# Issuing the split of a feed-forward unit's second weights with priority

## The chip, the cores and the metric

The kernel runs on one core of one Trainium2 chip. The metric is the device time of one launch in microseconds. A core has a matrix engine (PE, which loads weights in a queue of its own, PEld, beside its matmuls), two elementwise engines (DVE, the vector engine, and ACT, the scalar engine), POOL (GpSimd) and SP (which issues DMAs here). Each engine works through its own instructions in order, and semaphores join them.

## The reference, cut to what matters

Two decoder layers over 512 tokens of width 1024. Each layer has a feed-forward unit, a token mixer (differential attention in the first layer, causal pooling in the second), a cross-attention into 256 memory tokens, and a second feed-forward unit; a layer norm follows each. So there are four feed-forward units:

```python
def swiglu_ffn(x, w_in, w_out):
    h = x @ w_in                      # (512, 1024) @ (1024, 5632)
    g, u = jnp.split(h, 2, axis=-1)
    return (jax.nn.silu(g) * u) @ w_out   # (512, 2816) @ (2816, 1024)

x = layer_norm(a * x + 0.5 * swiglu_ffn(x, ffn_w_in[i, 0], ffn_w_out[i, 0]), ...)
```

All is in float32. The change touches the feed-forward units alone.

## The kernel before, in words

**Numbers in two halves.** PE multiplies numbers of a rounded format (fp32r). An operand is split in two: ACT casts it to the high half (`wh` for weights), DVE subtracts that from the operand and writes the low half (`wl`). A product is three matmuls per block (`mm3`): high by high (L230), then the low half of the activations by the high weights or the like (L231), then the low weights (L232). So the third matmul of a product needs DVE's `wl`, while the first two need only ACT's `wh`. The pairs `wh`/`wl` have four buffers, handed out in turn.

**A feed-forward unit** (`ffn`) works through eleven blocks of 256 hidden columns in five turns (`FFN_TURNS`): three blocks in the first turn, two in each of the others. The blocks of a turn are called lanes. Each 2 x 2 block product of a lane (`up`) is computed with seven products in place of eight, in the manner of Strassen. Its results stand in PSUM banks `x`, `y` and `z`. The first product of a lane takes the weights `ra` and goes to `x`; the second takes the weights `rc` and goes to `y`; the third takes `ra` again, which POOL's accumulating DMA has turned into a sum by then, and goes to `z`; and so on. ACT copies `x` to `sp`, and DVE adds `y` to it (`hr`, L819).

Beside the lanes of a turn run the products of the way down (`down`) of two blocks of an earlier turn: `b` weights are split like the others (L142, L143), the activations are `ha` and `hb` (`seven` makes them of `hr`, with the sums `sr` in L883 to L886), the results stand in banks `px` and `py`, and DVE adds them to the tokens (`X<-X,px`, L930), which frees the bank. Each tag of banks has two.

`up`, `down` and the rest are generators. `ffn` advances them in turn, so that the program's text order is lane by lane within a step. The recording layer then places the instructions on each engine in an order that it works out from this text order, the dependencies and its priorities. A block under `tc.high_priority()` ranks ahead of what was recorded earlier and is not placed yet; `issue_after` holds an instruction behind a given one.

In `up`, `operand` makes the split of a raw tile: the cast in L742, the subtraction in L744. The variable `v2` holds the split of the second weights, `rc`. In a unit's first turn, lane 0 makes it early, ahead of its first product (`early > 1`); every other lane makes it at the point where `y` begins. `at_start` is true in the first turn of the kernel's first unit only.

Of the kernel before, what the change touches and what calls it, by code (L numbers as in the profile page):

```python
# [125 lines left out]
class Trunk:  # L126
# [592 lines left out]
    def up(self, w, u, lane, early, between):  # L719
# [11 lines left out]
        def load(tag, *block):  # L731
            t = self.raw_tile((4, H), tag)
            self.last_load = nc.sync.dma_start(t, source(*block))
            return t
# [4 lines left out]
        def operand(raw, *behind):  # L739
            v = self.hl([P, 4, H])  # L740
            with self.after([act for act, _ in behind]):
                hi = nc.scalar.copy(v[0], raw)  # L742
            with self.after([dve for _, dve in behind]):
                lo = nc.vector.tensor_sub(v[1], raw, v[0].bitcast(F32))  # L744
            splits.append((hi, lo))
            return v
# [30 lines left out]
        third = lane == 2  # L777
        at_start = early > 0 and self.begins is None
# [5 lines left out]
        rc = load("rc", 2, 1)  # L784
# [11 lines left out]
        v2 = early > 1 and operand(rc, *((self.turned,) if at_start else ()))  # L796
# [8 lines left out]
        nc.scalar.copy(p1, x)  # L805
        yield
        y = bank(self.aux("y", yz))
        v2 = v2 or operand(rc, *((self.made_parts,) if third and at_start else ()))
        with self.behind() if at_start else nullcontext():
            if early > 1 and not at_start:  # L810
                wide = v2[0][:, :2].rearrange("p k n -> p (k n)")
# [988 lines left out]
```

## Time and profile before

| | |
|---|---|
| median of 3 runs | 1905.58 us (1904.58 to 1907.38) |
| the profiled execution | 1907.98 us, its span 1906.2 us |
| PE busy | 1892.1 us (99%), 13136 matmuls |
| weight loads busy | 1733.3 us (91%) |
| DVE busy | 1549.4 us (81%) |
| ACT busy | 1004.8 us (53%) |
| granted clock of PE | 0.999 of full speed |

The times of rows count from the span's start. A matmul's shown duration is longer than its share of PE, since matmuls overlap: how fast PE goes is read from the distance of starts. The four feed-forward units lie in about the first 305 us, from 737 to 1062 us, from 1062 to 1388 us, and from 1574 us to the end.

### The profile page before, as it was taken

What the parts mean: (1) busy time and instruction counts of PE and PEld (TensorE: products, weight loads), DVE (VectorE), ACT (ScalarE), POOL (GpSimd) and SP (SyncE); (2) the same over time, 40 slices, a digit from 0 to 9 for tenths busy, and PEclk for the clock granted to TensorE, in tenths of its full rate; (3) what the DMA queues carried; (4) which work ended last, traced back from release to release, by engine and by line L of the source; (5) the groups of instructions that cost most, each with busy time, mean ns of one, the idle gap of its engine ahead of it and who ended that gap; (6) DMA issues with size and microseconds to landing.
All of it is one profiled execution on the core that took longest, in us unless ns stands there. A gap on an engine that the chain in (4) does not pass through costs nothing.

```text
span 1906.2 us, 32584 instructions
## 1 busy us (share of the span) xinstructions
PE 1892.1 (99%) x13136; PEld 1733.3 (91%) x13136; DVE 1549.4 (81%) x2250; ACT 1004.8 (53%) x1546; POOL 318.0 (17%) x274
## 2 busy tenths in 40 slices
PE   9999999999999999999999999999999999999998
PEld 8999998888889988999998999999899889999996
DVE  7888989888876558889887988898797568998886
ACT  6555553566654436555554655555455436555552
POOL 3112120111210002221220311212130012211210
PEclk9999999999999999999999999999999999999999
DMA  9978772322225327987784687878344438867861
GB/s 250 216 166 185 166 143 89 103 67 70 97 67 177 111 66 185 192 177 166 149 185 165 121 178 166 182 165 184 101 133 136 143 75 178 179 154 169 188 132 54
DMA packets 246871, 277.96 MB, mean 146 GB/s; under 512 B 8384, under 2 KB 212672, under 8 KB 246720
## 3 DMA queue, kind: packets, MB, share of 16 engines
q0 software_dynamic: 92928, 92.29, 31.5%
q1 hardware_dynamic: 153792, 183.59, 29.8%
q8 instruction: 103, 1.69, 0.3%
q14 instruction: 48, 0.39, 0.1%
HBM read 273.75 MB, written 2.10 MB: 145 GB/s over the span
## 4 chain that ended last, share of the span: by engine, by line
PE 88%; DVE 8%; DMA 2%; ACT 1%; issue 1%; POOL 0%; SPq 0%; DVEq 0%; ACTq 0%; POOLq 0%
PE x L230 7%; PE x L231 7%; PE x L232 7%; PE z L230 4%; PE z L231 4%; PE z L232 4%; PE ps L230 4%; PE ps L232 4%; PE ps L231 4%; PE px L230 2%; PE px L232 2%; PE px L231 2%; PE y L232 2%; PE x L769 2%; PE y L230 2%; PE y L231 2%
## 5 line engine op out<-in xcount | busy, mean ns | idle before, releaser
L737 POOL DMA_DIRECT2D ra<-in_ffn_w_in_dram x132 | 170.7, 1314 | 983.1 <-DVE wl L744 824.7
L742 ACT CAST wh<-ra 128x1024 fp32r<-128x1024 f32 x176 | 185.1, 1053 | 209.6 <-PE x L231 68.3
L744 DVE TENSOR_TENSOR wl<-ra,wh 128x1024 fp32r<-128x1024 f32 x176 | 214.0, 1220 | 67.5 <-ACT wh L742 67.1
L230 PE MATMUL x<-xe,wh 128*128 128x256 f32 x704 | 195.1, 277 | 0.0
L231 PE MATMUL x<-xe,wh 128*128 128x256 f32 x704 | 195.0, 277 | 0.0
L232 PE MATMUL x<-xe,wl 128*128 128x256 f32 x704 | 194.9, 277 | 0.0
L742 ACT CAST wh<-rc 128x1024 fp32r<-128x1024 f32 x132 | 139.0, 1053 | 102.6 <-PE x L231 41.6
L142 ACT CAST wh<-b 128x1024 fp32r<-128x1024 f32 x112 | 117.8, 1052 | 132.9 <-PE x L231 68.0
L744 DVE TENSOR_TENSOR wl<-rc,wh 128x1024 fp32r<-128x1024 f32 x132 | 159.9, 1219 | 25.1 <-ACT wh L742 25.1
L143 DVE TENSOR_TENSOR wl<-b,wh 128x1024 fp32r<-128x1024 f32 x112 | 136.7, 1220 | 41.3 <-ACT wh L142 41.3
L230 PE MATMUL x<-xh,wh 128*128 128x256 f32 x536 | 148.8, 278 | 0.0
L231 PE MATMUL x<-xl,wh 128*128 128x256 f32 x536 | 148.4, 277 | 0.0
L232 PE MATMUL x<-xh,wl 128*128 128x256 f32 x536 | 148.4, 277 | 0.0
L231 PEld LDWEIGHTS x<-xe,wh 128*128 128x128 f32 x704 | 132.3, 188 | 1.3
L230 PEld LDWEIGHTS x<-xe,wh 128*128 128x128 f32 x704 | 132.1, 188 | 1.3
L232 PEld LDWEIGHTS x<-xe,wl 128*128 128x128 f32 x704 | 132.6, 188 | 0.0
L143 DVE TENSOR_TENSOR wl<-raw,wh 128x1024 fp32r<-128x1024 f32 x64 | 81.4, 1281 | 42.8 <-ACT wh L142 42.2
L231 PEld LDWEIGHTS x<-xl,wh 128*128 128x128 f32 x536 | 100.8, 188 | 0.7
L230 PEld LDWEIGHTS x<-xh,wh 128*128 128x128 f32 x536 | 100.6, 188 | 0.7
L232 PEld LDWEIGHTS x<-xh,wl 128*128 128x128 f32 x536 | 100.9, 188 | 0.0
L142 ACT CAST wh<-raw 128x1024 fp32r<-128x1024 f32 x64 | 66.6, 1050 | 60.8 <-PE xq L231 16.8
L230 PE MATMUL z<-xe,wh 128*128 128x256 f32 x352 | 97.6, 277 | 0.0
(447 smaller groups left out, 6261.8 us busy)
## 6 DMA issues: line engine op xcount, KB each, us to landing
ra<-in_ffn_w_in_dram POOLq DMA_DIRECT2D x132, 512.0 KB, 6.8
rc<-in_ffn_w_in_dram SPq DMA_DIRECT2D x88, 512.0 KB, 5.7
b<-in_ffn_w_out_dram SPq DMA_DIRECT2D x76, 512.0 KB, 4.8
ra<-in_ffn_w_in_dram SPq DMA_DIRECT2D x44, 512.0 KB, 4.7
rc<-in_ffn_w_in_dram POOLq DMA_DIRECT2D x44, 512.0 KB, 6.8
raw<-in_xa_wkv_dram SPq DMA_DIRECT2D x16, 1024.0 KB, 5.5
raw<-in_da_w_qkv_dram SPq DMA_DIRECT2D x24, 512.0 KB, 3.7
raw<-in_xa_wq_dram SPq DMA_DIRECT2D x8, 1024.0 KB, 5.2
```

The source lines that it names most:

```text
L142: self.nc.scalar.copy(hi, src),
L143: self.nc.vector.tensor_sub(lo, src, hi.bitcast(F32)),
L230: self.first_mm = mm(out, w[0], x[0], start=start, stop=False, skip_group_check=again)
L231: mm(out, w[0], x[1], start=False, stop=False, skip_group_check=again)
L232: self.last_mm = mm(out, w[1], x[0], start=False, stop=stop, skip_group_check=again)
L737: nc.gpsimd.dma_start(t, source(*block), accum_op=ALU.add)
L742: hi = nc.scalar.copy(v[0], raw)
L744: lo = nc.vector.tensor_sub(v[1], raw, v[0].bitcast(F32))
L769: self.last_mm = nc.tensor.matmul(ps[:, j], v[i][:, k, j * P : (j + 1) * P], x[l][:, k], start=n == i == l == 0, stop=n == 7 and i == 1, s ...
```

## The change

The split of `rc` (cast and subtraction) that a lane makes where its `y` begins is recorded under `high_priority()`, except in the first turn of the first unit. Nothing else is touched.

```diff
         y = bank(self.aux("y", yz))
-        v2 = v2 or operand(rc, *((self.made_parts,) if third and at_start else ()))
+        with self.tc.high_priority() if not v2 and not at_start else nullcontext():
+            v2 = v2 or operand(rc, *((self.made_parts,) if third and at_start else ()))
         with self.behind() if at_start else nullcontext():
```

In `up`, `early` is 0 in all turns but the first, where it is 2, 1 and 1 for the three lanes; `at_start` inside `up` is `early > 0 and self.begins is None`, which holds in the first unit's first turn. The added line moves the later lines of the file down by one (L819 becomes L820, L930 becomes L931). SP's and POOL's instructions stand in the same order as before.

The rows below are the order in which the engines' instructions stand in the program; numbers behind names tell buffers apart. The place is the turn that begins near 188 us of the profile, the fourth of the first unit. `rc_1947` and `rc_1951` are the second weights of its two lanes, `wl_2319` and `wl_2351` the low halves of their splits, `y_2317` and `y_2349` their results.

DVE before, from the last `hb` of the turn before to the first `hr` of this one:

```order
L914 TENSOR_TENSOR b1_1953<-b1_1953,b3_1957 128x1024
L143 TENSOR_TENSOR hb_2156<-hr_1724,hb_2155 128x256
L143 TENSOR_TENSOR hb_2156<-sr_2159,hb_2155 128x1024
L744 TENSOR_TENSOR wl_2319<-rc_1947,wh_2318 128x1024
L883 TENSOR_TENSOR sr_2205<-hr_1756 128x256
L886 TENSOR_TENSOR sr_2205<-hr_1756 128x256
L884 SCALAR_TENSOR_TENSOR sr_2205<-sr_2205,hr_1756 128x256
L930 SCALAR_TENSOR_TENSOR X0_74<-X0_74,px_2301 128x512
L885 SCALAR_TENSOR_TENSOR sr_2205<-sr_2205,hr_1756 128x256
L930 SCALAR_TENSOR_TENSOR X1_75<-X1_75,px_2309 128x512
L744 TENSOR_TENSOR wl_2351<-rc_1951,wh_2350 128x1024
L819 TENSOR_TENSOR hr_2346<-y_2317,sp_2262 128x2x256
```

DVE now, at the same place, from eight rows further up:

```order
L931 SCALAR_TENSOR_TENSOR X2_76<-X2_76,px_1679 128x512
L143 TENSOR_TENSOR hb_1580<-sr_1583,hb_1579 128x1024
L744 TENSOR_TENSOR wl_2319<-rc_1947,wh_2318 128x1024
L143 TENSOR_TENSOR hb_1580<-hr_1119,hb_1579 128x256
L744 TENSOR_TENSOR wl_2351<-rc_1951,wh_2350 128x1024
L884 TENSOR_TENSOR sr_2159<-hr_1724 128x256
L887 TENSOR_TENSOR sr_2159<-hr_1724 128x256
L885 SCALAR_TENSOR_TENSOR sr_2159<-sr_2159,hr_1724 128x256
L931 SCALAR_TENSOR_TENSOR X3_77<-X3_77,px_1687 128x512
L886 SCALAR_TENSOR_TENSOR sr_2159<-sr_2159,hr_1724 128x256
L915 TENSOR_TENSOR b1_1953<-b1_1953,b3_1957 128x1024
L143 TENSOR_TENSOR hb_2156<-hr_1724,hb_2155 128x256
```

The two subtractions have moved up, the first by nine rows and the second by fourteen; the rows between them and the common `hr_2346` are the same, one or two 1024-wide rows later.

PE before, at the border of the two lanes' `y`:

```order
L231 MATMUL y_2317<-xl_86,wh_2318 128x256
L232 MATMUL y_2317<-xh_84,wl_2319 128x256
L230 MATMUL y_2349<-xh_84,wh_2350 128x256
L231 MATMUL y_2349<-xl_86,wh_2350 128x256
L230 MATMUL py_2385<-wh_2381,ha_1577 128x512
L232 MATMUL y_2349<-xh_84,wl_2351 128x256
```

PE now, at the end of the second lane's `y`:

```order
L230 MATMUL y_2349<-xh_84,wh_2350 128x256
L231 MATMUL y_2349<-xl_86,wh_2350 128x256
L232 MATMUL y_2349<-xh_84,wl_2351 128x256
L230 MATMUL py_2385<-wh_2381,ha_1577 128x512
L231 MATMUL py_2385<-wl_2382,ha_1577 128x512
```

The one `py` matmul that stood ahead of the second lane's first low product now stands with the other `py` matmuls, behind all of that lane's `y`. PE's order changes in this way at eight places (the third and the fourth turn of each unit) and nowhere else.

ACT before, in the same turn:

```order
L142 CAST hb_1579<-sr_1583 128x1024
L142 CAST hb_1579<-hr_1119 128x256
L742 CAST wh_2318<-rc_1947 128x1024
L142 CAST hb_2155<-hr_1724 128x256
L742 CAST wh_2350<-rc_1951 128x1024
L805 COPY sp_2262<-x_2237 128x512
L142 CAST hb_2155<-sr_2159 128x1024
L142 CAST wh_2381<-b2_1955 128x1024
```

ACT now:

```order
L142 CAST hb_1579<-sr_1583 128x1024
L742 CAST wh_2318<-rc_1947 128x1024
L142 CAST hb_1579<-hr_1119 128x256
L142 CAST hb_2155<-hr_1724 128x256
L742 CAST wh_2350<-rc_1951 128x1024
L805 COPY sp_2262<-x_2237 128x512
L142 CAST wh_2381<-b2_1955 128x1024
L142 CAST hb_2155<-sr_2159 128x1024
```

The first cast of `rc` has passed one small row, and the cast of `hb` that needs DVE's `sr_2159` has gone behind the cast of `b2`.

## The prediction

> **What bounds the kernel now.** I read the page's first and fourth part, then the waits of the weight loads, then the chain of waits, and last the timelines around each place that it names.
>
> ```profile
> span 1906.2 us, 32584 instructions
> ...
> PE 1892.1 (99%) x13136; PEld 1733.3 (91%) x13136; DVE 1549.4 (81%) x2250; ACT 1004.8 (53%) x1546; POOL 318.0 (17%) x274
> ...
> PE 88%; DVE 8%; DMA 2%; ACT 1%; issue 1%; POOL 0%; SPq 0%; DVEq 0%; ACTq 0%; POOLq 0%
> ```
>
> PE is busy for 99% of the span, and 88% of the chain that ended last is PE itself. A change that removes no matmul can win only what PE loses between matmuls. The 8% of DVE in the chain is not such a loss: while the chain runs through DVE, PE goes on with matmuls that it has ready. The loss itself stands in the list of waits, of the weight loads (who waited <- for whom: total us, times, longest), and the chain says where DVE is last (start, us, what; the first and the last of seven such rows, one for each of the seven waits):
>
> ```profile
> PEld y L232 <- DVE wl L744: 3.2, 7, 0.5
> PEld q L230 <- issue: 2.6, 7, 0.4
> ...
> 199.47 1.15 DVE wl L744
> ...
> 1760.30 1.14 DVE wl L744
> ```
>
> The first row is the largest wait of the weight loads, and it is the one that the change is about: the low half `wl` of the second lane's `rc` weights comes too late for its `y`. It bounds what can be won there: 3.2 us, 0.17% of the span. It includes the time in which the previous matmul still runs, so the true loss is read from the starts of PE's matmuls (timeline: start, us, engine, line, operation) at the first and the last place:
>
> ```profile
> 200.01 0.28 PE L231 MATMUL y<-xl,wh 128*128 128x256 f32 x1
> 200.13 0.39 PE L230 MATMUL py<-wh,ha 128*128 128x512 f32 x1
> 200.66 0.19 PEld L232 LDWEIGHTS y<-xh,wl 128*128 128x128 f32 x1 [0.46 <-DVE wl L744]
> 200.66 0.39 PE L232 MATMUL y<-xh,wl 128*128 128x256 f32 x1
> 200.89 0.28 PE L230 MATMUL y<-xh,wh 128*128 128x256 f32 x1
> ...
> 203.36 0.40 PE L231 MATMUL py<-wl,ha 128*128 128x512 f32 x1
> 203.59 0.40 PE L232 MATMUL py<-wh,ha 128*128 128x512 f32 x1
> ...
> 1760.84 0.28 PE L231 MATMUL y<-xl,wh 128*128 128x256 f32 x1
> 1760.96 0.39 PE L230 MATMUL py<-wh,ha 128*128 128x512 f32 x1
> 1761.49 0.38 PE L232 MATMUL y<-xh,wl 128*128 128x256 f32 x1
> 1761.71 0.28 PE L230 MATMUL y<-xh,wh 128*128 128x256 f32 x1
> ```
>
> From start to start, a 256-column matmul takes 0.12 us (200.01 to 200.13; 0.11 at 1760.84) and a 512-column one 0.23 (203.36 to 203.59). So the `y` at 200.66 could have started at 200.13 + 0.23 = 200.36: 0.30 us late. It then takes 0.23 to the next start instead of 0.11 to 0.12, since its weight load starts with it (200.66, released by DVE's `wl`): another 0.11. At the last place it is 1761.49 - 1761.19 = 0.30, and 0.22 - 0.11 = 0.11. The eighth place, the first unit's third turn, just makes it:
>
> ```profile
> 142.52 0.40 PE L230 MATMUL py<-wh,ha 128*128 128x512 f32 x1
> 142.76 0.36 PE L232 MATMUL y<-xh,wl 128*128 128x256 f32 x1
> 142.96 0.28 PE L230 MATMUL y<-xh,wh 128*128 128x256 f32 x1
> ```
>
> There the wait is 0.24 - 0.23 = 0.01, and the slow restart 0.20 - 0.11 = 0.09.
>
> **The change part by part.** It adds and removes no instruction, and SP's and POOL's orders are the same in both programs, so no DMA is issued past another. Under priority now are 38 pairs of a cast (ACT) and a subtraction (DVE): two in each of the sixteen later turns, two in each of the three first turns that are not the first unit's. They make four kinds of place.
>
> *Middle turns (third and fourth of each unit, eight places).* DVE's and ACT's rows of before, and the PE matmul that needs the bank that DVE frees:
>
> ```profile
> 189.48 1.05 ACT L742 CAST wh<-rc 128x1024 fp32r<-128x1024 f32 x1
> 191.02 1.06 ACT L742 CAST wh<-rc 128x1024 fp32r<-128x1024 f32 x1 [0.18 <-ACT hb L142]
> ...
> 189.70 1.22 DVE L143 TENSOR_TENSOR hb<-sr,hb 128x1024 fp32r<-128x1024 f32 x1
> 190.84 0.42 DVE L143 TENSOR_TENSOR hb<-hr,hb 128x256 fp32r<-128x256 f32 x1
> 192.18 0.68 DVE L930 SCALAR_TENSOR_TENSOR X<-X,px 128x512 f32<-128x512 f32 x1
> 195.72 1.22 DVE L744 TENSOR_TENSOR wl<-rc,wh 128x1024 fp32r<-128x1024 f32 x1
> 199.39 1.22 DVE L744 TENSOR_TENSOR wl<-rc,wh 128x1024 fp32r<-128x1024 f32 x1
> 200.53 0.68 DVE L819 TENSOR_TENSOR hr<-y,sp 128x512 f32<-128x512 f32 x1
> 201.13 1.21 DVE L143 TENSOR_TENSOR wl<-b,wh 128x1024 fp32r<-128x1024 f32 x1
> ...
> 195.78 0.39 PE L230 MATMUL px<-wh,ha 128*128 128x512 f32 x1
> ```
>
> Both casts are long done (192.08) when DVE comes to the second subtraction at 199.39: DVE's order, not ACT, makes `y` wait. In the new order the two subtractions stand right behind `hb<-sr` of 189.70 and behind `hb<-hr` of 190.84. A 1024-wide row occupies DVE for 1.14 (189.70 to 190.84), so the first runs 190.84 to 191.98 and ends its write at 192.06; `hb<-hr`, 0.34; the second starts at 192.32 (its cast ends at 192.08, 0.24 earlier) and ends at 193.54. PE reads it at 200.13 at the earliest: 6.6 us of slack in place of a wait of 0.30.
>
> What is paid: everything between is later by 2 x 1.14 = 2.28 at first. The first that PE needs is the `X<-X,px` of 192.18: it starts at 194.46 and ends at 195.14, and the product that reuses its bank starts at 195.78, so 0.64 us are left. The small `sr` and `hb` rows feed products of the next turn. ACT's second `hb<-sr` cast now stands behind a `wh<-b` and needs DVE's later `sr`; its product also belongs to the next turn. At 200.53 both orders have the same rows behind them, and DVE has had no gap, so `hr<-y` and `wl<-b` stay where they are. `wl<-b` ends at 201.13 + 1.21 = 202.34. PE wants it at 203.36, and 0.41 earlier now: 0.61 left. I cost the move at nothing here; the two covers are 0.64 and 0.61 us, and each is the next to be late.
>
> *Second turn of each unit (four places).* Here the splits stood early enough, and PE's order does not change. The first row that both orders have in common again is the `wl<-ra` of 84.27; ahead of it stands now the last `X<-X,px`, at 84.27 - 0.60 (the step from 200.53 to 201.13) = 83.67. Its bank is written next at 111.43. Nothing.
>
> ```profile
> 84.27 1.21 DVE L744 TENSOR_TENSOR wl<-ra,wh 128x1024 fp32r<-128x1024 f32 x1
> ...
> 111.43 0.40 PE L230 MATMUL px<-wh,hb 128*128 128x512 f32 x1
> ```
>
> *Last turn of each unit (four places).* One subtraction moves up by two rows' worth of `sr`, and ACT's `wh<-ra` of 252.58 goes behind a cast of 1.05 and a copy of 0.58:
>
> ```profile
> 251.27 1.05 ACT L142 CAST hb<-sr 128x1024 fp32r<-128x1024 f32 x1 [0.67 <-DVE sr L885]
> 252.58 1.06 ACT L742 CAST wh<-ra 128x1024 fp32r<-128x1024 f32 x1 [0.26 <-PE x L231]
> 256.04 0.68 DVE L819 TENSOR_TENSOR hr<-y,sp 128x512 f32<-128x512 f32 x1
> 257.89 0.28 PE L230 MATMUL z<-xh,wh 128*128 128x256 f32 x1
> ```
>
> The `sr` before the cast waits for the moved 1.14, so the cast starts near 252.4, the copy near 253.4, and `wh<-ra` near 253.9, ending about 255.0. DVE took that operand at 254.90, so `hr<-y` at 256.04 slips by 0.1. `z` at 257.89 needs its end (256.72): 1.0 us left. Nothing.
>
> *First turn of the second to fourth unit.* In the second and third unit the third lane's subtraction (748.04) goes ahead of two rows, which slip by 1.14. `xl<-pt` of 746.31 then ends near 748.1, and the `y` that waits for its bank starts at 751.07. In the fourth unit some five rows change places; I take nothing there and bound it by one wait of the kind above, 0.4 us:
>
> ```profile
> 746.31 0.68 DVE L143 TENSOR_TENSOR xl<-pt,xh 128x512 fp32r<-128x512 f32 x1
> 748.04 1.22 DVE L744 TENSOR_TENSOR wl<-rc,wh 128x1024 fp32r<-128x1024 f32 x1
> 751.07 0.28 PE L230 MATMUL y<-xh,wh 128*128 128x256 f32 x1
> ```
>
> **The sum.** Seven places at 0.30 + 0.11 = 0.41 make 2.9 us, the eighth 0.1: 3.0 us. Bounds of a place: nothing (the wait is replaced by another) and 0.46, the wait of the weight load. The profiled execution took 1907.98 us around its span of 1906.2; it becomes 1905.0. It stands 2.4 above the median of the runs, so against 1905.58 the forecast is 1902.6, 0.16% less.
>
> The restart term is where a rule differs. The Trainium skill, "TensorE: Matmul & The Clock Gate", section "Architectural detail", says that PE's queue can pull weight loads ahead of matmuls in flight; read so, a restart should cost nothing, and the sum would be 7 x 0.30 = 2.1. The trace does not agree at these places: the weight load of 200.66 reads the very `wl` that is awaited, and it starts with its matmul. I keep 0.11.
>
> **The rivals.**
> - *The stall only moves.* DVE is without a gap across the whole stretch, so what is put back may be late in its turn: `X<-X,px` or `wl<-b`. For it: covers of 0.64 and 0.61 us only, and two rows of 1.14 pass. Against it: both covers come out positive by rows. If one is eaten and a wait of about the old size appears, the time is 1905.6.
> - *Slower, by the bank of `px`.* If a further 1024-wide row (1.14) gets ahead of the `X` read, or a cast is that late, PE waits 1.14 - 0.64 = 0.50 and restarts for 0.11, at eight places: 4.9 us lost against 3.0 won, 1907.5. It decides from 0.64 + 0.27 = 0.9 us of lateness (8 x 0.38 = 3.0). The cast that DVE needs at 192.32 has only 0.24 to spare, which speaks for it; against it speaks that the same rows stand ahead of that cast on ACT as before.
> - *The restart is free.* Then only the waits go: 2.1 us, 1903.5. The rows at 200.66 and 1761.49 speak against it.
> - *More is won.* Operands freed earlier could also shorten waits that the change does not aim at, such as the `q` row in the list (2.6 us). To pass 0.2% it must add 0.8 us; no row of a feed-forward unit promises that. 1901.5.
>
> **How the numbers follow.** Forecast 0.55, stall moves 0.17, slower by the bank 0.10, free restart 0.10, more won 0.08. 0.2% is 3.8 us, about what a measurement of this kernel can tell from no change; the three runs of before lie 2.8 us apart (1904.58 to 1907.38), so a true 3.0 may be read as 2 or 4. Hence 0.17 for faster: all of the last case, and a sixth of the forecast's. The bank's case gives 0.08 for slower, less the part of it that stays small. The rest, 0.75, is the same. The range goes from 1900.9 (the forecast, read 1 us low, and most of the last case) to 1906.2 (the moved stall with scatter); it leaves out most of the slower case.
>
> **What would show it.** In the list of waits of the weight loads, `y` on `wl` L744 is gone or under 0.3 us. In the middle turns PE's `py` stands behind all 24 `y`, and starts follow each other by 0.11 to 0.12. DVE's second subtraction starts near 192.3 in that turn, and `px` at 195.78 has no wait. Wrong would be a wait of `px` on `X` L931, of `py` on `wl` L143, or a `wl` that waits for its cast `wh` at the new place.

## The result, and the profile after

| kernel | median, us | runs |
|---|---|---|
| before | 1904.97 (1903.94 to 1909.51) | 14 |
| changed | 1900.91 (1899.17 to 1902.06) | 14 |

The ratio is 0.9976, 95% interval 0.9969 to 0.9983: by the medians 4.1 us less, by the ratio 4.6 (0.24%; 3.2 to 5.9), where 3.0 (0.16%) was forecast. The profiled execution of the changed kernel took 1902.06 us around its span of 1900.3.

The page of the changed kernel: the span, the engines' busy time, and the shares of the chain that ended last:

```profile
span 1900.3 us, 32585 instructions
...
PE 1888.2 (99%) x13136; PEld 1732.6 (91%) x13136; DVE 1548.0 (81%) x2250; ACT 1003.0 (53%) x1546; POOL 317.8 (17%) x274
...
PE 94%; DVE 2%; DMA 1%; ACT 1%; issue 1%; POOL 0%; SPq 0%; DVEq 0%; ACTq 0%; POOLq 0%
```

PE is at 99% as before. The chain no longer runs through DVE (2% for 8%). The waits of the weight loads (who waited <- for whom: total us, times, longest), from the top of the list:

```profile
PEld q L230 <- issue: 2.6, 7, 0.4
PEld px L230 <- issue: 1.6, 4, 0.5
```

The row of `y` on `wl` L744, which headed the list of before with 3.2 us, is gone. The two rows that stood next below it are what they were (`q` 2.6 us in 7 times, `px` 1.6 in 4). The turn that the prediction worked through, on DVE and on PE (timeline: start, us, engine, line, operation):

```profile
189.37 1.22 DVE L744 TENSOR_TENSOR wl<-rc,wh 128x1024 fp32r<-128x1024 f32 x1
190.51 0.42 DVE L143 TENSOR_TENSOR hb<-hr,hb 128x256 fp32r<-128x256 f32 x1
190.84 1.22 DVE L744 TENSOR_TENSOR wl<-rc,wh 128x1024 fp32r<-128x1024 f32 x1
...
192.99 0.68 DVE L931 SCALAR_TENSOR_TENSOR X<-X,px 128x512 f32<-128x512 f32 x1
...
199.66 1.22 DVE L143 TENSOR_TENSOR wl<-b,wh 128x1024 fp32r<-128x1024 f32 x1
```

```profile
194.32 0.39 PE L230 MATMUL px<-wh,ha 128*128 128x512 f32 x1
...
198.66 0.28 PE L232 MATMUL y<-xh,wl 128*128 128x256 f32 x1
...
201.04 0.28 PE L232 MATMUL y<-xh,wl 128*128 128x256 f32 x1
201.15 0.39 PE L230 MATMUL py<-wh,ha 128*128 128x512 f32 x1
201.38 0.39 PE L231 MATMUL py<-wl,ha 128*128 128x512 f32 x1
```

This stretch lies 1.46 us earlier than in the profile of before (`px`: 195.78 there, 194.32 here). So DVE's second subtraction, at 190.84, stands at 192.30 in the time of before; 192.32 was forecast. It ends at 192.06, 6.6 us before the first `y` that reads it (198.66). All `y` follow one another without a gap, and `py` stands behind the last. `X<-X,px` ends at 193.67, 0.65 before `px` writes its bank (forecast 0.64). `wl<-b` ends at 200.88, 0.50 before `py` reads it (forecast 0.61). Neither cover was eaten.

Set matmul against matmul, the two profiled executions lie 5.9 us apart at the end. The seven places add 0.42 to 0.55 each, 3.2 in all. Another 1.5 us comes between 82 and 142 us, where PE waits for nothing in either trace and its matmuls simply follow each other more slowly in that of before. And 0.9 us comes between 716 and 726 us: in the profile of before PE waits there (0.58 us, at 721.45) for DVE's `X` of L377, which stands behind a split whose `ra` came in late; in the other it doesn't wait. Neither of these is a wait that the change aims at, and one pair of executions can't tell whether it causes them. So executions of the same program had to be compared.

### The profile page after: what moved, and what is told of

Read it like the earlier page. It is cut to its first block, busy times and chain, and to the rows that moved or that the text cites. A ratio compares the mean times of both kernels' runs of the same rounds, so it can differ in the third digit from the quotient of the medians.

```text
span 1900.3 us, 32585 instructions
## 1 busy us (share of the span) xinstructions
PE 1888.2 (99%) x13136; PEld 1732.6 (91%) x13136; DVE 1548.0 (81%) x2250; ACT 1003.0 (53%) x1546; POOL 317.8 (17%) x274
## 4 chain that ended last, share of the span: by engine, by line
PE 94%; DVE 2%; DMA 1%; ACT 1%; issue 1%; POOL 0%; SPq 0%; DVEq 0%; ACTq 0%; POOLq 0%
PE x L230 7%; PE x L231 7%; PE x L232 7%; PE z L230 4%; PE z L231 4%; PE z L232 4%; PE ps L230 4%; PE ps L232 4%; PE ps L231 4%; PE px L232 3%; PE px L230 3%; PE px L231 3%; PE x L769 3%; PE y L231 2%; PE y L230 2%; PE y L232 2%
## 5 line engine op out<-in xcount | busy, mean ns | idle before, releaser
L744 DVE TENSOR_TENSOR wl<-ra,wh 128x1024 fp32r<-128x1024 f32 x176 | 214.5, 1221 | 62.5 <-ACT wh L742 61.8
L744 DVE TENSOR_TENSOR wl<-rc,wh 128x1024 fp32r<-128x1024 f32 x132 | 159.7, 1219 | 25.0 <-ACT wh L742 24.8
L143 DVE TENSOR_TENSOR wl<-b,wh 128x1024 fp32r<-128x1024 f32 x112 | 136.8, 1221 | 41.4 <-ACT wh L142 41.4
L143 DVE TENSOR_TENSOR wl<-raw,wh 128x1024 fp32r<-128x1024 f32 x64 | 81.4, 1281 | 42.9 <-ACT wh L142 40.2
```

Source lines behind the costliest of these rows:

```text
L143: self.nc.vector.tensor_sub(lo, src, hi.bitcast(F32)),
```

## The experiments

The expectations name three theories; the third was drawn up from the first four of the runs below. S, seven waits: the prediction's seven places, and the rest is scatter. X: the change itself is worth 4 us or more, since it shortens the stretch in which PE runs slowly. N, nine waits: beside the seven, the eighth place (the first unit's third turn) and one in the first unit's second turn, which the prediction costed at nothing. Kernels with the same figure for before ran on the same chip, beside the same runs of it. Gains in us are worked out from the ratio, on 1905.

| kernel | priority for | median, us | before, us | ratio, 95% interval |
|---|---|---|---|---|
| e_null | nothing (before again) | 1905.88 | 1906.29 | 0.9997 (0.9988 to 1.0006) |
| e_again | as changed | 1901.89 | 1906.29 | 0.9976 (0.9967 to 0.9986) |
| e_sub | the subtraction alone | 1902.19 | 1906.29 | 0.9981 (0.9970 to 0.9992) |
| e_cast | the cast alone | 1906.65 | 1906.29 | 0.9999 (0.9991 to 1.0008) |
| e_second | second turns | 1906.72 | 1905.36 | 1.0005 (0.9996 to 1.0014) |
| e_middle | middle turns | 1902.67 | 1905.36 | 0.9989 (0.9979 to 0.9999) |
| e_pad_before | nothing, four matmuls added | 1907.15 | 1905.36 | 1.0005 (0.9997 to 1.0014) |
| e_pad_after | as changed, four matmuls added | 1907.59 | 1905.36 | 1.0009 (1.0000 to 1.0018) |
| e_later | later turns | 1902.41 | 1905.99 | 0.9984 (0.9976 to 0.9993) |
| e_lane1 | second lane, later turns | 1902.94 | 1905.99 | 0.9982 (0.9973 to 0.9991) |
| e_lane0 | first lane, later turns | 1905.91 | 1905.99 | 0.9998 (0.9989 to 1.0007) |
| e_all | all turns | 1902.64 | 1905.99 | 0.9984 (0.9976 to 0.9993) |
| e_again2 | as changed | 1902.12 | 1906.80 | 0.9973 (0.9963 to 0.9983) |
| e_skip | as changed, less the first unit's second turn | 1903.60 | 1906.80 | 0.9984 (0.9975 to 0.9993) |
| e_first | first turns of units 2 to 4 | 1907.18 | 1906.80 | 1.0001 (0.9992 to 1.0010) |
| e_skip2 | as e_skip | 1902.90 | 1906.79 | 0.9983 (0.9973 to 0.9993) |
| e_nomid | as changed, less the middle turns | 1906.39 | 1906.79 | 0.9996 (0.9988 to 1.0005) |

**The same two programs again** (e_null: the priority replaced by `nullcontext()`; e_again: the changed kernel).

> The kernel before, built again with an empty context in place of the priority. Its time should be that of before within 1 us, which shows the scatter of a comparison. It is there for the profile. Theory S (the seven waits of y are worth 3.0 us, the rest of the 4.1 us between the medians and of the 5.9 us between the two profiled spans is scatter in places that the change does not touch): the stretch at the start in which 256-column matmuls follow each other by 0.118 instead of 0.113 us ended at 143 us in the profile of before and at 81 us in that of after; S expects it to end at another place here, and the 0.74 us wait of PE near 720 us to be absent or of another size. Theory X (the change itself is worth 4 us or more, because it also shortens that slow stretch): it ends near 143 us again.

> The changed kernel again. S: 3 us faster than before (ratio 0.9984), the slow stretch ends at a place that differs from 81 us; the seven waits are absent again. X: 4 us or more (0.9979 or less), and the slow stretch ends near 81 us again.

The gain came out again (0.9976), and the program of before, run again, differs from itself by nothing that can be told (0.9997). What tells most is the profile of e_null. The list of weight-load waits of this second execution of the program of before:

```profile
PEld y L232 <- DVE wl L744: 4.7, 9, 1.1
```

Nine waits for the seven of the first profile, and 4.7 us for 3.2. The ninth is in the first unit's second turn, in the first lane's `y`. It stands on DVE and on PE of e_null:

```profile
78.30 1.22 DVE L744 TENSOR_TENSOR wl<-rc,wh 128x1024 fp32r<-128x1024 f32 x1
```

```profile
78.31 0.28 PE L230 MATMUL y<-xh,wh 128*128 128x256 f32 x1
78.43 0.28 PE L231 MATMUL y<-xl,wh 128*128 128x256 f32 x1
79.58 0.39 PE L232 MATMUL y<-xh,wl 128*128 128x256 f32 x1 [0.87 <-DVE wl L744]
79.80 0.28 PE L230 MATMUL y<-xh,wh 128*128 128x256 f32 x1
```

From 78.43 the next start should be at 78.55, and comes at 79.58: 1.03 late, and 0.11 more for the restart (0.22 to the next start). The same place in the profile of before that the prediction was made from, on PE and on DVE:

```profile
80.63 0.28 PE L231 MATMUL y<-xl,wh 128*128 128x256 f32 x1
80.75 0.28 PE L232 MATMUL y<-xh,wl 128*128 128x256 f32 x1
```

```profile
77.85 1.22 DVE L744 TENSOR_TENSOR wl<-rc,wh 128x1024 fp32r<-128x1024 f32 x1
```

There the subtraction ended at 79.07, 1.7 us ahead of its `y`. DVE's order is the same; the subtraction came 0.45 earlier, and PE 2.2 us later. Set matmul against matmul, PE had lost 0.6 of these by 30 us, in small waits at the start, and lost 1.6 more between 36 and 78 us. How it could do so without waiting shows in the windows of both (window, sum, PE busy with its matmuls, granted clock, DMA share, GB/s). Of before, then of e_null:

```profile
40.00:70.00 30.00, 30.00 (x257) 1.00 1.16 268
```

```profile
40.00:70.00 30.00, 30.00 (x267) 1.00 1.16 271
```

In the same 30 us PE did 267 matmuls in e_null and 257 in before, both at a granted clock of 1.00 and both 100% busy. In before this longer step lasted from 35 to 143 us, in e_null it ended at 26. So X falls as the whole account: the program of before runs without the long step too, and its time is not that of the changed one. The changed order takes the new wait away. In e_again2, a later execution of the changed kernel that has no long step either (267 matmuls in the same window), PE comes to this `y` only 0.12 us later than in e_null, and finds its `wl` written. On DVE (both lanes' subtractions in one row) and on PE:

```profile
76.02 2.35 DVE L744 TENSOR_TENSOR wl<-rc,wh 128x1024 fp32r<-128x1024 f32 x2
```

```profile
78.55 0.28 PE L231 MATMUL y<-xl,wh 128*128 128x256 f32 x1
78.67 0.28 PE L232 MATMUL y<-xh,wl 128*128 128x256 f32 x1
```

As a part of the account X stays open. The profile of e_again did what X expected and not what S did: its long step ends at 81 us again, and its ratio is 0.9976. The change doesn't set the step off: it is there between 40 and 70 us in before, the changed kernel, e_again and e_lane1, ahead of the first rows that the change moves (and in e_all, which moves earlier rows as well). But in the changed kernel, e_again and e_lane1 it ends some four matmuls into the first lane's `y` of the second turn, while in before and in e_all it runs on past that `y`. One such profile of the old order can't tell whether the change helps to end it.

**Which half of the pair does it** (e_sub and e_cast: the priority put around one instruction of `operand` alone).

```
-                hi = nc.scalar.copy(v[0], raw)
+                with self.tc.high_priority() if first else nullcontext():   # e_cast
+                    hi = nc.scalar.copy(v[0], raw)
...
+                with self.tc.high_priority() if first else nullcontext():   # e_sub
+                    lo = nc.vector.tensor_sub(v[1], raw, v[0].bitcast(F32))
```

> Priority for the subtraction (DVE) alone, not for the cast (ACT). PE's order is that of the changed kernel. If DVE's order is the cause, as the prediction has it, the seven waits are gone and the time is that of the changed kernel within 1 us. Rival (the cast has to be early too): the subtraction at its new place waits for its cast, and part of the waits come back: 1 to 3 us slower than the changed kernel.

> Priority for the cast (ACT) alone. PE's order is that of before, and DVE's almost. If DVE's order is the cause, the seven waits of 0.3 us stay and the time is that of before within 1 us. Rival (ACT's cast is what matters): 3 us faster.

The subtraction alone keeps the gain within its interval, and the cast alone brings none. In e_sub no `y` waits for `wl`; in e_cast, whose line numbers stand one higher, all nine do:

```profile
PEld y L232 <- DVE wl L745: 4.2, 9, 0.5
```

So it is DVE's order, as forecast.

**Which turns** (the condition of the priority). `u` counts a unit's blocks of 256 columns: 3 and 4 are in the second turn, 5 to 8 in the two middle ones.

```
-        with self.tc.high_priority() if not v2 and not at_start else nullcontext():
+        with self.tc.high_priority() if not v2 and u in (3, 4) else nullcontext():          # e_second
+        with self.tc.high_priority() if not v2 and u in (5, 6, 7, 8) else nullcontext():    # e_middle
```

> Priority in the second turn of each unit only. PE's order is that of before. Theory N (in most executions before has nine waits, not seven: besides the eight middle turns, the first lane's y of the first unit's second turn waits 0.5 to 1.1 us; the profiled execution of before hid it, since its PE ran at 0.118 us per 256-column matmul up to 143 us): about 0.8 us faster than before, the eight waits of the middle turns stay (3.3 us in the weight loads' list), the one near 79 us is gone. Theory S (seven waits, the rest scatter): time of before within 0.3 us.

> Priority in the third and fourth turn of each unit only. PE's order is that of the changed kernel. N: about 3.3 us faster than before; the wait near 79 us stays where the slow pitch has ended before it (0.5 to 1.1 us), and is absent where it has not. S: 3.0 us faster, as the whole change.

The profiles did what N says: e_second lists eight waits, 3.7 us, with the one near 79 us gone; e_middle keeps that one alone:

```profile
78.42 0.28 PE L231 MATMUL y<-xl,wh 128*128 128x256 f32 x1
79.11 0.39 PE L232 MATMUL y<-xh,wl 128*128 128x256 f32 x1 [0.41 <-DVE wl L744]
```

Here it is 79.11 - 78.54 = 0.57, and not 1.03. The times of e_middle (2.1 us less, interval 0.2 to 4.0) agree with eight places. Those of e_second don't bear out the 0.8 us that N expects: no gain, 0.8 at most. Beside e_null, its profiled execution lost 1.5 us between 20 and 24 us, in a wait of `x` for its cast, ahead of everything that the edit moves.

**Four matmuls more** ahead of that `y` (0.92 us, their result overwritten), to make PE late there on purpose.

```
+            if u == 3 and self.ln_at is None:
+                wide = v2[0][:, :2].rearrange("p k n -> p (k n)")
+                for _ in range(4):
+                    nc.tensor.matmul(
+                        y.rearrange("p j n -> p (j n)"), v2[0][:, 0, :P], wide, start=True, stop=True
+                    )
```

> The kernel before with four more 512-column matmuls (0.92 us of PE) ahead of the first lane's y in the second turn of the first unit; they need the cast only, and y overwrites what they write. N: where PE runs at the fast pitch there, it would have waited anyway for wl, so the four cost 0.1 to 0.5 us and not 0.92, and the wait near 79 us shrinks by as much. S (no wait at that place): 0.9 us slower than before.

> The same four matmuls in the changed kernel. Both theories: no wait is there to take them in, so 0.9 us slower than the changed kernel, 3.1 us faster than before by N, 2.1 by S.

This failed as a test. In e_pad_before the wait near 79 us is gone, but in both kernels the four matmuls set off the long step: from 79 to 143 us in e_pad_before, and from 79 to 300 in e_pad_after. The windows of e_pad_after, ahead of and behind the place:

```profile
40.00:70.00 30.00, 30.00 (x267) 1.00 1.16 269
...
150.00:190.00 40.00, 40.00 (x284) 1.00 0.87 192
```

The second window holds 293 matmuls in before, in e_null and in the changed kernel. So e_pad_after came out 1.7 us above before, and 6 above where the changed kernel stands, not 0.9: the long step costs more than the wait that was to be priced, and hides it.

**Later turns, lanes, all turns** (e_later, e_lane1, e_lane0, e_all). `early` is above zero in a unit's first turn, `at_start` holds in the first block's.

```
+        with self.tc.high_priority() if not v2 and not early else nullcontext():                  # e_later
+        with self.tc.high_priority() if not v2 and not early and lane == 1 else nullcontext():    # e_lane1
+        with self.tc.high_priority() if not v2 and not early and lane == 0 else nullcontext():    # e_lane0
+        with self.tc.high_priority() if not v2 else nullcontext():                                # e_all
```

> Priority in the sixteen later turns only; the three first turns of the second to fourth unit are left as in the kernel before. Nine waits (eight middle ones at 0.42 us and the one of the first unit's second turn at 0.6 to 1.1): all of them lie in later turns, so the whole gain of the changed kernel is kept, about 4.1 us, ratio 0.9978. Rival: the first turns carry what the seven or eight middle places do not explain; then only 3.0 to 3.3 us are kept, 0.9984. No row of PE should show y waiting for wl L744, and the splits of the first turns are where they were before.

> Priority for the second lane's split alone, in later turns. PE's order is the changed kernel's. Nine waits: the eight middle waits are all of the second lane and go, 8 x 0.42 = 3.3 us, ratio 0.9983; the wait near 79 us is the first lane's and stays (0.46 to 1.03 plus 0.11), unless PE runs slowly up to there. Rival (both splits must move to win anything, since the second one queues behind the first): the waits stay at 0.3 and the ratio is 1.000.

> Priority for the first lane's split alone, in later turns. PE's order is that of before. Nine waits: the eight middle waits stay (the list of weight-load waits shows eight, about 0.46 us each), and only the one near 79 us goes: 0 to 1.1 us faster, ratio 0.9994 to 1.000. Rival (the first lane's split alone is enough, since DVE then reaches the second one earlier): the whole 4.1 us, 0.9978; by DVE's order the second one has the same rows ahead of it as before, so the rival should fall.

> The changed kernel with priority in the first turn of the first block as well. One subtraction of 1.14 us there goes ahead of hr<-y and hb<-xh,xl, and one cast ahead of a copy of 0.58; PE's order is the same. Nine waits: nothing of it lies in a later turn, so 0.9978, give or take what the start scatters (0.0005). Rival A: the split of that turn is late too (PE waits up to 0.8 us at 25 us in the start): 0.4 us better, 0.9976. Rival B: hr<-y being 1.1 us later delays the next product of the start: 0.5 to 1.1 us worse, 0.9982.

The second lane's split carries the middle turns: e_lane1 gains 3.4 us, 3.3 expected, and e_lane0 0.4, with eight waits of 3.7 us left in its list. e_later came out at 3.0, which is the rival's number; the 4.1 expected lies inside its interval (1.3 to 4.6). In e_lane1's profile the wait near 79 us, which it leaves in place, doesn't occur: PE had the long step up to 80 us. e_all came out at 0.9984 where 0.9978 was expected, close to its rival B (0.9982); its interval holds both. No version was found that beats the changed kernel.

**The first turns, and the second turn left out** (e_again2, e_skip, e_first, then e_skip2 and e_nomid).

```
+        with ... if not v2 and not at_start and not (self.ln_at is None and u in (3, 4)) else ...   # e_skip, e_skip2
+        with ... if not v2 and not at_start and early else ...                                      # e_first
+        with ... if not v2 and not at_start and u not in (5, 6, 7, 8) else ...                      # e_nomid
```

> The changed kernel again, beside the two others of this call. Eight middle waits and, in a part of the executions, the one near 79 us are gone: 3.3 to 4.1 us faster than before, ratio 0.9978 to 0.9983. No wait of y for wl L744 in its profile.

> The change in all its turns but the first unit's second. Nine waits: the eight middle ones are gone, the one near 79 us is back (0.46 to 1.03 us plus 0.11 in the profile, unless PE runs at its slow pitch up to there), so the time lies 0.5 to 1.1 us above the changed kernel of the same call. Rival (that turn is worth nothing, as the prediction had it): the time of the changed kernel within 0.3 us.

> Priority in the first turns of the second to fourth unit alone; PE's order is that of before. Nine waits: every wait of y for wl L744 stays (eight rows of about 0.46 us, and the one near 79 us where PE isn't slow), and the time is that of before, ratio 1.000. Rival: these turns carry the 0.8 us that the middle waits don't explain, ratio 0.9996, with a wait of the profile of before gone in the first turn of a unit.

> The change in all its turns but the first unit's second, a second time, for its profile. Nine waits: one row of y for wl L744 near 79 us, of 0.46 to 1.1 us (none, if PE runs at its slow pitch up to there), and none at the middle places; 3.0 to 3.5 us faster than before, ratio 0.9982 to 0.9984. Rival (that turn is worth nothing): the changed kernel's 0.9973 to 0.9976.

> The change in all its turns but the middle ones; PE's order is that of before. Nine waits: the eight middle rows stay, the one near 79 us goes; 0.5 to 1.1 us faster than before, ratio 0.9994 to 0.9998. Rival (the rest of the gain comes with the middle turns): ratio 1.000 or above.

The first turns bring nothing (e_first 1.0001, nine waits in its list). Without the second turn of the first unit the gain is 3.0 and 3.2 us, beside 5.1 for the changed kernel on the same chip as the first of them: 2.1 us apart, where N expected 0.5 to 1.1. (The profiled execution of e_skip has a span of 6852.4 us, beside a median of 1903.60 of its runs, so its rows are not read; e_skip2 is the same kernel.) e_nomid gains 0.8, as N has it, within an interval of -1.0 to 2.3. Its list shows the eight middle waits and no ninth:

```profile
PEld y L232 <- DVE wl L744: 3.7, 8, 0.5
```

e_skip2 missed one expectation: its wait near 79 us didn't come, on DVE and on PE:

```profile
78.60 1.22 DVE L744 TENSOR_TENSOR wl<-rc,wh 128x1024 fp32r<-128x1024 f32 x1
```

```profile
79.96 0.30 PE L232 MATMUL y<-xh,wl 128*128 128x256 f32 x1
```

The subtraction ends at 79.82, and PE had lost 1.3 us beside e_null by 25 us (in waits of `x` and `y` for their casts), so it came just behind it.

## Why the prediction was right in its mechanism and short in its sum

*The seven places: right.* From e_null to e_again2, matmul against matmul, PE's lead grows by 0.42 to 0.43 at seven of the eight middle places, and by 0.55 at one. A wait of 0.30 to 0.32 and a restart of 0.11 are at these places in each trace that has the wait (198.37 in e_null: 0.30 and 0.11). So the rival with a free restart falls. The Trainium skill, "TensorE: Matmul & The Clock Gate", section "Architectural detail", says that PE's queue can pull weight loads ahead of matmuls in flight. At none of these places did that make the restart free (0.11 us each time); there the load reads the very operand that is awaited.

*The eighth place: mis-sized.* "Just makes it", 0.1 us, was true of one execution. In e_null it is 0.31 + 0.11 = 0.42 (140.46 us), and e_cast, e_second, e_lane0, e_first and e_nomid all have the same. It was near zero only in the two profiles, before and e_pad_before, whose PE had the long step up to 143 us. Add 0.3.

*The second turn of each unit: the step that failed.* "Here the splits stood early enough", with "Nothing" as its price, was read from rows of a single execution, in which PE came late to the first unit's second turn. The prediction worked out no cover for that `y`; it looked at the bank of `px` alone. Seven profiles of kernels that leave the first lane's split there where it was show the wait as 1.14, 0.69, 0.62 and 0.57 us with its restart (e_null, e_middle, e_first, e_cast), and as nothing in three (before, e_lane1, e_skip2): 0.43 in the mean. The other three units have none in any profile. So the sum becomes 8 x 0.42 + 0.43 = 3.8 us, from 3.4 where PE comes late to 4.5 where it doesn't. The three comparisons of the changed kernel gave 4.6, 4.6 and 5.1 us, with 3.8 inside each interval. That all three lie above it, by 0.8 and more, isn't explained: scatter, the whole ninth wait (1.1) in most executions, and a long step that ends earlier under the change would each do it, and no run tells them apart. That e_sub, e_later and e_all, which free the same nine places, gain 3.6, 3.0 and 3.0 speaks for scatter.

How much of this the times alone show: the four kernels that free the middle places but leave the second turn's first lane (e_middle, e_lane1, e_skip, e_skip2) gain 2.1 to 3.4, 2.9 in the mean, against 3.4 from the rows. The three that do the second turn without the middle (e_second, e_lane0, e_nomid) gain -1.0, 0.4 and 0.8. The eight middle places are thus shown both ways: without them nothing clear of noise is left, and with them most of the gain. The six that move the second lane's and the first lane's splits in all later turns (the changed kernel three times, e_sub, e_later, e_all) gain 3.0 to 5.1, 4.0 in the mean, 1.1 more than the four. So the ninth is shown in the traces, and in them the change takes it away; by the times it lies between nothing and some 1.1 us, and its size stays open.

*DVE's order and not ACT's cast: right* (e_sub, e_cast). *Last turns, and first turns of the later units, at nothing: not contradicted* (e_first gains nothing; no kernel moved the last turns alone). *The covers: right*, at 0.65 and 0.50 us, so the moved stall and the slower case by the bank of `px` fall: the lists of the changed kernel show no wait of `px` on `X` L931 and none of `py` on `wl` L143. *More won:* the time came near that case, but not by the wait that it named; the `q` row didn't move.

*The line of 0.2%.* 0.2% is 3.8 us. The forecast lay 0.8 on one side of it, the medians 0.3 on the other. With the eighth place at its full size and the second turn taken as a chance and not as nothing, the forecast would have been 3.8 us, on the line itself, with faster and the same about even.

## What to carry to other kernels

A cover of 1.7 us that one profiled execution shows is worth no more than the steadiness of what runs ahead of it: before a step is costed at nothing, ask what ends the cover if the waiting engine comes as early as its matmul count allows, and put a chance on it. Where an engine has no gap ahead of a wait that it causes, as DVE here, the wait is won by the order of its work; look first at which long row could go last without being missed. And a second profile of the unchanged program is the cheapest experiment there is: here it showed at once the wait that the prediction had put at nothing.

## What the runs showed of the hardware that was not expected

At one and the same granted clock (1.00) PE keeps one of two steps from matmul to matmul. With 256 columns it is 0.113 us (199.00 to 200.02 in the changed kernel: nine steps in 1.02) or 0.118 (44.77 to 48.42 in before: 31 in 3.65); the two windows of 40 to 70 us above, 267 matmuls and 257, give the same 4%. The Trainium skill, "TensorE: Matmul & The Clock Gate", section "Wait — 56ns, not 53.3ns?", gives one figure at the full clock: columns over 2.4 GHz plus some 2.5 ns. By it the step would be an estimated 0.109 us. Both steps measured here are longer than that. The long step began behind a restart of PE in before (35.24 us), and behind the four added matmuls in the two padded kernels. It ended within a microsecond behind the restart near 142.7 us in before and in e_pad_before, at some 81 us, without a wait, in the changed kernel, and at the unit's end at 300 us in e_pad_after and e_all. The profiled execution of e_all, with it from 36 to 301 us, has a span of 1908.1, though its runs have a median of 1902.64. What sets it off stays open; it wasn't tried apart. In that execution it is worth some 7 us: matmul against matmul, e_all falls 7.2 us behind e_later between 36 and 301 us. That is more than the change.
